# Splitting 28 weight slabs early and pairing two heads in a fused two-block kernel

## The chip, the cores and the metric

The kernel runs on one core of one Trainium2 chip. The metric is the device time of one execution in microseconds. Three executions of the kernel before took 2578.41, 2578.83 and 2579.85 us; their median, 2578.83 us, is the time to compare with.

## The reference

One launch computes two blocks, one after the other, on a sequence of 512 tokens of width 1024, in float32. Cut to what matters here:

```python
for layer in range(2):                                   # block 1
    p = rms_norm(x, norm_g[layer]) @ w_in[layer]
    c_q, c_kv, k_r, gate_a, dil_qkv, gate_b = split(p)
    a = mla_attention(...) * silu(gate_a)
    b = dilated_attention(dil_qkv, cos, sin) * silu(gate_b)
    x = x + concatenate([a, b]) @ w_out[layer]           # output projection
x = rms_norm(x, final_g)
for l in range(2):                                       # block 2
    h = rmsnorm(x) * (1 + scale) + shift
    if l == 0:                                           # recurrent mixers
        p = h @ ab_w_in                                  # 2560 + 1920 columns
        mix = concatenate([hgrn2(p...), rwkv7(p...)]) @ ab_w_out
    else:
        mix = concatenate([fourier(h...), conformer(h...)]) @ cd_w_out
    x = x + gate * mix
    x = x + gate * conv_ffn(rmsnorm(x) * (1 + scale) + shift)
```

The dilated attention has 8 heads of width 64. Each head attends in three groups (dilations 1, 4 and 16), each with its own softmax, and the three results are weighted by a softmax over their log sums.

## The kernel before

Activations lie transposed: features on the 128 partitions, the 512 tokens along the free dimension. A product with a weight matrix goes slab by slab: a slab is 1024 x 128 weights, 512 KB, held as a 128 x 8 x 128 tile. To keep float32 accuracy each operand is split into two parts of the type fp32r (high and low), and three products are summed (`mm3`, L130 to L132). So a slab costs one DMA into `wraw` on SP's queue (L67), a copy on ACT that makes `whi` (L75), a subtraction on DVE that makes `wlo` (L76), and 24 matmuls of 128x512 (`gemm`). `wraw`, `whi` and `wlo` have three buffers each.

Block 1 runs two layers. In each, `block1_mixers` computes the latent attention, then the dilated one. For each pair of dilated heads `operands(p)` makes queries and keys with six gemms, with a rotation of which one multiplication lies on GpSimd (POOL, L591). `attention(p)` then treats the two heads one after the other: for four query tiles, score matmuls into `sc` (L620 to L623), a masked maximum on DVE, an exponential on ACT; then a small exchange of maxima and sums (`ot`, `fa`); then the probabilities are scaled by the factor `fa` on DVE (L663), transposed on TensorE against the identity (`tp`, L669, L671), copied by ACT into `pt` (L674 to L678) and multiplied with the values into `po` (L683, L688).

Each layer ends in `out_proj`: eight gemms with `w_out`, each added to `xT`. In layer 0 each new tile of `xT` is scaled and split into `hh` and `hl` for the next layer's gemms (`Scaled.tile`). In layer 1 the last two gemms go in halves into `pl`, and the norm for block 2 follows (`Norm`).

In block 2 the function `m2` holds the recurrent mixers. Of their slabs, 12 of `w_rw` (the r, k and v of four head pairs) and 16 of `w_hg` go through `gemm` like any other, in between the small matmuls of the recurrences.

A scheduler of the framework puts each engine's instructions in an order while the program is built, by priority and by its own idea of durations; the tile pools add the waits for buffers. On the chip each engine keeps to that order, and so does SP's queue of DMA issues: an instruction that waits holds up all that stands behind it on its engine.

Of the kernel before, what the change touches and what calls it, by code (L numbers as in the profile page):

```python
# [12 lines left out]
ALU = mybir.AluOpType  # L13
# [11 lines left out]
class Ctx:  # L25
# [161 lines left out]
    def out_proj(self, pool, W, k0, mix, xcol, gate=None, norm=None, parts=None):  # L187
        for _ in self.out_proj_steps(pool, W, k0, mix, xcol, gate, norm=norm, parts=parts):
            pass
# [44 lines left out]
def at(x, k):  # L234

    return x[k] if isinstance(x, list) else x[:, k, :]

# [178 lines left out]
def block1_mixers(c, l, nm, mixf, side, w0, fill):  # L416
# [4 lines left out]
    if True:  # L421
# [114 lines left out]
        with ExitStack() as e2:  # L536
# [42 lines left out]
            def operands(p):  # L579

                q0, k0 = (dp.tile([128, 2, S], F32R, name=n, tag=n, bufs=2) for n in ("q0", "k0"))
                k0l = dp.tile([128, S], F32R, name="k0l", tag="k0l", bufs=2)
                qk12 = dp.tile([128, 2, 2, S], F32, name="qk12", tag="qk12", bufs=2)
                qk[p] = q0, k0, k0l, qk12
                for gi in range(3):
                    for j in range(2):
                        ps = c.gemm(I["w_dqk"][l][:, 6 * p + 2 * gi + j], hh, hl)
                        sh = c.t2("shf")
                        xr = c.t2("xr")
                        nc.vector.stream_shuffle(sh, ps, SHUF)  # L590
# [14 lines left out]
                        yield  # L605

            def attention(p):
                q0, k0, k0l, qk12 = qk.pop(p)
                po = c.pz.tile([128, S], F32, name="po", tag="pz")
                for e in range(2):  # L610
                    eb = slice(64 * e, 64 * e + 64)
                    hcol = slice(128 * p + 64 * e, 128 * p + 64 * e + 64)
                    st = dp.tile([128, 2, 2, 4], F32, name="st", tag="st", bufs=2)
                    nm = dp.tile([128, 2, 4], F32, name="nm", tag="nm", bufs=2)
                    pp = dp.tile([128, 4, S], F32, name="pp", tag="pp", bufs=2)
                    for i in range(4):
                        w0 = (0, 64, 192, 256)[i]
                        sc = c.px.tile([128, S], F32, name="sc", tag="px")
                        tq = slice(128 * i, 128 * i + 128)
                        nc.tensor.matmul(sc[:, 0:256], lhsT=q0[:, e, tq], rhs=k0[:, e, w0:w0 + 256], start=True, stop=False)  # L620
                        nc.tensor.matmul(sc[:, 0:256], lhsT=q0[eb, e, tq], rhs=k0l[eb, w0:w0 + 256], start=False, stop=True)
                        for gi in range(2):
                            nc.tensor.matmul(sc[:, 256 + 128 * gi:384 + 128 * gi], lhsT=qk12[eb, 0, gi, tq],  # L623
                                             rhs=qk12[eb, 1, gi, tq], start=True, stop=True)
                        for z in range(2):
                            w = slice(256 * z, 256 * z + 256)
                            nc.vector.tensor_tensor_reduce(pp[:, i, w], in0=sc[:, w], in1=dmask[:, 4 * z or i, :], scale=1.0, scalar=3 * NEG,
                                                           op0=ALU.add, op1=ALU.max, accum_out=st[:, 0, z, i:i + 1])
                        nc.vector.tensor_scalar(nm[:, :, i], st[:, 0, :, i], -0.125, None, op0=ALU.mult)  # L629
                        for z in range(2):  # L630
                            pz = pp[:, i, 256 * z:256 * z + 256]
                            nc.scalar.activation(pz, pz, AF.Exp, bias=nm[:, z, i:i + 1], scale=0.125,  # L632
                                                 accum_out=st[:, 1, z, i:i + 1])

                    ex = dp.tile([128, 2, 2, 128], F32, name="ex", tag="ex", bufs=2)
                    bc = lambda t: t.rearrange("p (z o n) -> p z o n", z=1, o=1).to_broadcast([128, 2, 4, 32])
                    nc.vector.tensor_tensor(ex[:, 0].rearrange("p z (i n) -> p z i n", i=4),
                                            st[:, :, 0, :].rearrange("p z (i o) -> p z i o", o=1).to_broadcast([128, 2, 4, 32]),
                                            bc(sel[:, 0:32]), op=ALU.mult)
                    nc.vector.tensor_tensor(ex[:, 1].rearrange("p z (n r) -> p z r n", r=4),  # L640
                                            st[:, :, 1, :].rearrange("p z (i o) -> p z i o", o=1).to_broadcast([128, 2, 4, 32]),
# [7 lines left out]
                    nc.vector.tensor_tensor(M, st[:, 0], ot[:, 0], op=ALU.max)  # L649
                    nc.vector.tensor_tensor(e1, st[:, 0], M, op=ALU.subtract)  # L650
                    nc.vector.tensor_tensor(e2_, ot[:, 0], M, op=ALU.subtract)
                    nc.scalar.activation(fa[:, 1:3], fa[:, 1:3], AF.Exp, scale=0.125)
                    nc.vector.tensor_tensor(f, e1, st[:, 1], op=ALU.mult)
# [3 lines left out]
                    nc.vector.tensor_tensor(f, f, e1, op=ALU.mult)  # L657

                    pts = []
                    for i in range(4):  # L660
                        for z in range(2):
                            pz = pp[:, i, 256 * z:256 * z + 256]
                            nc.vector.tensor_scalar(pz, pz, f[:, z, i:i + 1], None, op0=ALU.mult)  # L663

                        blocks = (((0, 0, 64, 0), (64, 0, 128, 1)), ((0, 0, 128, 1), (128, 0, 128, 2)),
                                  ((0, 0, 128, 2), (128, 0, 128, 3)), ((192, 64, 64, 0), (64, 0, 128, 3)))[i]
                        tp = c.py.tile([128, 4, 128], F32, name="tp", tag="py")
                        for j, (o, r0, n, vt) in enumerate(blocks):
                            nc.tensor.transpose(tp[0:n, j, :], pp[:, i, o:o + n], c.ident)  # L669
                        for j in range(2):  # L670
                            nc.tensor.transpose(tp[:, 2 + j, :], pp[:, i, 256 + 128 * j:384 + 128 * j], c.ident)  # L671
                        pt = dp.tile([128, 4, 128], F32, name="pt", tag="pt", bufs=4)
                        if i in (1, 2):
                            nc.scalar.activation(pt, tp, AF.Copy)  # L674
                        else:
                            r0 = blocks[0][1]
                            nc.scalar.activation(pt[r0:r0 + 64, 0, :], tp[0:64, 0, :], AF.Copy)
                            nc.scalar.activation(pt[:, 1:4, :], tp[:, 1:4, :], AF.Copy)  # L678
                        pts.append((pt, blocks))
                    for i in range(4):  # L680
                        pt, blocks = pts[i]
                        for j, (o, r0, n, vt) in enumerate(blocks):
                            nc.tensor.matmul(po[eb, 128 * i:128 * i + 128], lhsT=v0[r0:r0 + n, vt, hcol],  # L683
                                             rhs=pt[r0:r0 + n, j, :], start=i == 0 and j == 0, stop=False)
                    for i in range(4):
                        pt, _ = pts[i]
                        for j in range(2):
                            nc.tensor.matmul(po[eb, i::4], lhsT=v12[:, j, i, hcol], rhs=pt[:, 2 + j, :],  # L688
# [123 lines left out]
def rwkv_lora(c, rp, pp, R, hh, hl):  # L812
    nc, W = c.nc, c.ins["w_rw"]
    for ct, n in enumerate(("th", "ad", "gd")):
        ps = c.gemm(W[:, ct], hh, hl)
# [11 lines left out]
def rwkv_g(c, rp, pp, R, P, hh, hl):  # L827

    out = []
    for j, n in enumerate("rkv"):  # L830
        ct = 3 + 3 * P + j
        ps = c.gemm(c.ins["w_rw"][:, ct], hh, hl)
# [396 lines left out]
def hgrn_fill(c, hh, hl, spill):  # L1229

    nc = c.nc
    for h in range(4):
# [13 lines left out]
        for z in (1, 2, 0, 3):  # L1246
            ps = c.gemm(c.ins["w_hg"][:, 4 * h + z], hh, hl)
# [340 lines left out]
def build(tc, I, out):  # L1588
    nc = tc.nc
    with ExitStack() as es:  # L1590
# [60 lines left out]


        for l in range(2):
            ex.close()
            prev = nm
            with ExitStack() as em:
# [15 lines left out]
                c.out_proj(mp, I["w_out"][l], 0, [mixf[:, k] for k in range(KD)], x, norm=nm)  # L1672
            xd = to_dram(xT)
        ea.close()

# [366 lines left out]
```

## Time and profile before

| | |
|---|---|
| median of three executions | 2578.83 us |
| the profiled execution's own time | 2578.49 us |
| its span | 2576.7 us |
| TensorE (PE) busy | 2488.2 us, 97% |
| VectorE (DVE) busy | 1643.1 us, 64% |
| ScalarE (ACT) busy | 1074.9 us, 42% |
| GpSimd (POOL) busy | 220.6 us, 9% |
| HBM read, written | 246.06 MB, 16.52 MB |

The span runs from the first instruction to the last; 1.8 us of the execution lie outside it. PE is the engine that is nearly always busy. The kernel's stages, in us from the span's start: layer 0 from 0 to about 545 (dilated attention 268 to 494, output projection 494 to 545), layer 1 to about 1070 (dilated attention 793 to 1018), the recurrent mixers to about 1600, then the first feed-forward part, the Fourier and convolution mixers and the second feed-forward part. All DMAs of the program are issued on SP's queue.

### The profile page before, as it was taken

Reading aid. Unit: us, or ns where it says so; the run is one execution under the profiler, and the core shown is the slowest. Engines: PE = TensorE matmul, PEld = TensorE weight load, DVE = VectorE, ACT = ScalarE, POOL = GpSimd, SP = SyncE. Lnnn points to the kernel's source line nnn. Section 1 sums busy time; section 2 is a strip of 40 time slices with the busy share of each in tenths; the row PEclk is TensorE's granted clock in tenths of the full one; section 3 lists DMA queues with packets and bytes.
Section 4 is the critical chain, followed back from the end, with each engine's and each line's share of the span. In section 5 each row is a group of like instructions: output and inputs, shape, how many; then the busy total and the mean of one; then the engine's idle time right before and its main releaser. Section 6 shows DMA issues by size and latency. Waiting matters only on the chain. (4 is left out here: it accounts for less than half of the span.)

```text
span 2576.7 us, 38952 instructions
## 1 busy us (share of the span) xinstructions
PE 2488.2 (97%) x15261; PEld 1999.1 (78%) x15261; DVE 1643.1 (64%) x3261; ACT 1074.9 (42%) x1947; POOL 220.6 (9%) x303
## 2 busy tenths in 40 slices
PE   8999999999999999999999888999999989999998
PEld 6769777787697777877677777878888767888887
DVE  5767666647677666576576575786444797543544
ACT  5653333526534335555434652532333424432331
POOL 0000111000001110211000130200000210100000
PEclk9999999999999999999999978999999989999999
DMA  4137121331271213321211422586333403233322
GB/s 150 45 127 241 54 58 56 109 111 40 93 278 58 58 58 95 105 74 51 88 48 55 143 81 82 190 269 209 101 88 122 149 1 97 80 88 103 96 83 81
DMA packets 92023, 265.09 MB, mean 103 GB/s; under 512 B 14528, under 2 KB 27072, under 8 KB 90944
## 3 DMA queue, kind: packets, MB, share of 16 engines
q1 hardware_dynamic: 91840, 262.61, 32.5%
q8 instruction: 120, 1.97, 0.3%
q14 instruction: 63, 0.52, 0.1%
HBM read 246.06 MB, written 16.52 MB: 102 GB/s over the span
## 5 line engine op out<-in xcount | busy, mean ns | idle before, releaser
L75 ACT ACTIVATE whi<-wraw 128x1024 fp32r<-128x1024 f32 (+3 forms) x370 | 348.5, 943 | 774.6 <-PE pg L131 563.7
L130 PE MATMUL pg<-hh,whi 128*128 128x512 f32 x1560 | 629.3, 403 | 7.9 <-ACT whi L124 6.6
L131 PE MATMUL pg<-hl,whi 128*128 128x512 f32 x1560 | 630.9, 404 | 0.0
L132 PE MATMUL pg<-hh,wlo 128*128 128x512 f32 x1560 | 628.0, 403 | 0.0
L76 DVE TENSOR_TENSOR wlo<-wraw,whi 128x1024 fp32r<-128x1024 f32 (+4 forms) x366 | 422.6, 1156 | 284.8 <-ACT whi L75 281.2
L130 PEld LDWEIGHTS pg<-hh,whi 128*128 128x128 f32 x1560 | 295.8, 190 | 88.0 <-ACT whi L124 6.6
L131 PEld LDWEIGHTS pg<-hl,whi 128*128 128x128 f32 x1560 | 295.8, 190 | 76.7 <-issue 8.1
L132 PEld LDWEIGHTS pg<-hh,wlo 128*128 128x128 f32 x1560 | 296.2, 190 | 71.6 <-issue 2.5
L132 PE MATMUL pg<-hidh,wlo 128*128 128x512 f32 (+1 forms) x396 | 145.5, 367 | 0.3 <-DVE wlo L76 0.3
L131 PE MATMUL pg<-hidl,whi 128*128 128x512 f32 (+1 forms) x396 | 145.6, 368 | 0.0
L130 PE MATMUL pg<-hidh,whi 128*128 128x512 f32 (+1 forms) x396 | 145.1, 366 | 0.0
L719 DVE CUSTOM_DVE_ANT_0 adaw<-adaw,sc 128x1024 f32<-128x1024 f32 x96 | 116.3, 1225 | 41.0 <-DMA adaw<-in_ada_w_dram 33.4
L591 POOL TENSOR_TENSOR shf<-shf,roped 128x512 f32<-128x512 f32 x48 | 62.0, 1292 | 532.7 <-ACT whi L75 249.2
L130 PE MATMUL pgv<-whi,hh 128*128 128x512 f32 (+1 forms) x240 | 89.7, 374 | 0.0
L132 PE MATMUL pgv<-whi,hl 128*128 128x512 f32 (+1 forms) x240 | 88.4, 368 | 0.0
L131 PE MATMUL pgv<-wlo,hh 128*128 128x512 f32 (+1 forms) x240 | 88.3, 368 | 0.0
L632 ACT ACTIVATE pp<-pp,nm 128x256 f32<-128x256 f32 x128 | 63.6, 497 | 54.9 <-DVE nm L629 54.8
L130 PEld LDWEIGHTS pg<-hidh,whi 128*128 128x128 f32 x396 | 74.3, 188 | 13.6 <-issue 0.4
L132 PEld LDWEIGHTS pg<-hidh,wlo 128*128 128x128 f32 x396 | 74.4, 188 | 13.1 <-DVE wlo L76 1.0
L131 PEld LDWEIGHTS pg<-hidl,whi 128*128 128x128 f32 x396 | 74.4, 188 | 12.7
L1529 ACT ACTIVATE fu<-fu 128x512 f32<-128x512 f32 x44 | 27.8, 631 | 112.2 <-DVE fu L745 112.2
L231 DVE SCALAR_TENSOR_TENSOR xT<-pg,mod,xT 128x512 f32<-128x512 f32 (+1 forms) x54 | 38.2, 710 | 48.5 <-PE pg L132 48.4
(512 smaller groups left out, 4486.2 us busy)
## 6 DMA issues: line engine op xcount, KB each, us to landing
adaw<-in_ada_w_dram SPq DMA_DIRECT2D x96, 512.0 KB, 4.6
wraw<-in_ffn_up_dram SPq DMA_DIRECT2D x88, 512.0 KB, 3.6
wraw<-in_w_dqk_dram SPq DMA_DIRECT2D x48, 512.0 KB, 3.6
wraw<-in_ffn_down_dram SPq DMA_DIRECT2D x32, 512.0 KB, 3.6
wraw<-in_w_dv_dram SPq DMA_DIRECT2D x24, 512.0 KB, 3.7
wraw<-in_w_gate_dram SPq DMA_DIRECT2D x16, 512.0 KB, 3.7
wraw<-in_w_out_dram SPq DMA_DIRECT2D x16, 512.0 KB, 3.7
wraw<-in_w_hg_dram SPq DMA_DIRECT2D x16, 512.0 KB, 3.7
```

The lines of the kernel that those rows point to most:

```text
L75: nc.scalar.activation(hi, raw, AF.Copy)
L76: (eng or nc.vector).tensor_tensor(lo, raw, hi.bitcast(F32), op=ALU.subtract)
L130: mm(out, lhsT=ah, rhs=bh, start=first, stop=False)
L131: mm(out, lhsT=ah, rhs=bl, start=False, stop=False)
L132: mm(out, lhsT=al, rhs=bh, start=False, stop=last)
L231: self.nc.vector.scalar_tensor_tensor(x, in0=ps, scalar=gate[:, o:o + 1], in1=x, op0=ALU.mult, op1=ALU.add)
L591: nc.gpsimd.tensor_tensor(sh, sh, roped[:, 1, :], op=ALU.mult)
L632: nc.scalar.activation(pz, pz, AF.Exp, bias=nm[:, z, i:i + 1], scale=0.125, accum_out=st[:, 1, z, i:i + 1])
L719: nc.vector.tensor_tensor_reduce(w, in0=w, in1=sc, scale=1.0, scalar=0.0, op0=ALU.mult, op1=ALU.add, accum_out=mod[:, j:j + 1])
L1529: nc.scalar.activation(u, u, AF.Silu)
```

## The change

Two things change together.

**Slabs split ahead.** A new class `Parts` stands for a slab that is split ahead of its use. `make` loads the raw slab into a tile `praw`, splits it into `phi` (ACT) and `plo` (DVE), and stores both to DRAM with two DMAs of 512 KB from GpSimd's queue. The three tiles have two buffers each, in a pool `pre` of their own. `out_proj` in block 1 calls `ahead` after each of its steps, which makes two slabs: 18 of the 28 in layer 0, 10 in layer 1. In `m2` the gemms that use these slabs load `whi` and `wlo` with two DMAs on SP's queue, and ACT and DVE have no part in it.

**Dilated heads.** `attention` treats the two heads of a pair together: their score matmuls, and later their value matmuls, alternate. The factor is no longer multiplied into the probabilities by DVE: ACT makes a diagonal matrix `dg` of it (two per query tile and head), and a matmul with `dg` as moving operand takes the place of the transpose. `pt` now lies in the memory of the probabilities, unused rows are set to zero by GpSimd (L717), and the value matmuls always use all 128 rows. The rotation's multiplication moves from GpSimd to DVE.

```diff
     def wslab(self, src, shape, raw=None, eng=None, out=None):
+        if isinstance(src, Parts):
+            hl = out or [self.w.tile(shape, F32R, name=t, tag=t) for t in ("whi", "wlo")]
+            for t, z in zip(hl, src.parts):
+                nc.sync.dma_start(t.bitcast(F32), z)
+            return hl
...
         for _ in self.out_proj_steps(pool, W, k0, mix, xcol, gate, norm=norm, parts=parts):
-            pass
+            if ahead is not None:
+                ahead()
...
+class Parts:
+    def __init__(self, c, src, name):
+        self.src = src.rearrange("p k n -> p (k n)")
+        self.parts = [c.dram.tile([128, 1024], F32, name=f"{name}{z}") for z in "hl"]
+
+    def make(self, c, pool):
+        raw = pool.tile([128, 1024], F32, name="praw", tag="praw", bufs=2)
+        c.nc.sync.dma_start(raw, self.src)
+        hl = [pool.tile([128, 1024], F32R, name=t, tag=t, bufs=2) for t in ("phi", "plo")]
+        c.split(*hl, raw)
+        for z, t in zip(self.parts, hl):
+            c.nc.gpsimd.dma_start(z, t.bitcast(F32))
...
-                        nc.gpsimd.tensor_tensor(sh, sh, roped[:, 1, :], op=ALU.mult)
+                        nc.vector.tensor_tensor(sh, sh, roped[:, 1, :], op=ALU.mult)
...
+                    sc = [c.px.tile([128, S], F32, name="sc", tag="px") for _ in es]
...
+                    for e, eb, _ in es:
+                        nc.tensor.matmul(sc[e][:, 0:256], lhsT=q0[eb, e, tq], rhs=k0l[eb, w0:w0 + 256], start=False, stop=True)
+                    for gi in range(2):
+                        for e, eb, _ in es:
+                            nc.tensor.matmul(sc[e][:, 256 + 128 * gi:384 + 128 * gi], lhsT=qk12[eb, 0, gi, tq],
                                              rhs=qk12[eb, 1, gi, tq], start=True, stop=True)
...
-                            pz = pp[:, i, 256 * z:256 * z + 256]
-                            nc.vector.tensor_scalar(pz, pz, f[:, z, i:i + 1], None, op0=ALU.mult)
+                            nc.scalar.activation(dg[:, z], c.ident, AF.Copy, scale=fs[e][:, z, i:i + 1])
...
-                            nc.tensor.transpose(tp[:, 2 + j, :], pp[:, i, 256 + 128 * j:384 + 128 * j], c.ident)
+                            mm(tp[:, 2 + j, :], lhsT=pp[e, i][:, 256 + 128 * j:384 + 128 * j], rhs=dg[:, 1], start=True, stop=True)
...
+                for i in range(4):
+                    for j in range(2):
+                        for e, eb, hcol in es:
+                            nc.tensor.matmul(po[eb, i::4], lhsT=v12[:, j, i, hcol], rhs=pts[e, i][0][:, 2 + j, :],
                                              start=False, stop=i == 3 and j == 1)
...
-            ps = c.gemm(c.ins["w_hg"][:, 4 * h + z], hh, hl)
+            ps = c.gemm(c.rparts[15 + 4 * h + z].cut(128), hh, hl)
...
+                pre = c.pool(em, "pre", B)
+                def ahead():
+                    for _ in range(2):
+                        if rtodo:
+                            rtodo.pop(0).make(c, pre)
-                c.out_proj(mp, I["w_out"][l], 0, [mixf[:, k] for k in range(KD)], x, norm=nm)
+                c.out_proj(mp, I["w_out"][l], 0, [mixf[:, k] for k in range(KD)], x, norm=nm, ahead=ahead)
```

What this does to the order of the instructions is seen at three places. First, ACT in the output projection of layer 0, before:

```order
L75 ACTIVATE whi<-wraw 128x1024
L361 ACTIVATE hh<-xT,gv 128x512
L370 ACTIVATE sqa<-xT 128x512
L75 ACTIVATE whi<-wraw 128x1024
L361 ACTIVATE hh<-xT,gv 128x512
L370 ACTIVATE sq<-xT 128x512
L75 ACTIVATE whi<-wraw 128x1024
```

And now (L75 has become L80, L361 L389, L370 L398; L129 is the copy in `split`):

```order
L129 ACTIVATE phi<-praw 128x1024 x2
L80 ACTIVATE whi<-wraw 128x1024
L389 ACTIVATE hh<-xT,gv 128x512
L398 ACTIVATE sqa<-xT 128x512
L129 ACTIVATE phi<-praw 128x1024
L80 ACTIVATE whi<-wraw 128x1024
L129 ACTIVATE phi<-praw 128x1024
L389 ACTIVATE hh<-xT,gv 128x512
L398 ACTIVATE sq<-xT 128x512
L80 ACTIVATE whi<-wraw 128x1024
```

The 18 copies of layer 0 stand between the copies that make `whi` for the projection's gemms and for the first three or four gemms of layer 1. The subtractions on DVE stand likewise.

Second, SP's queue at the same place, before:

```order
L67 DMA wraw<-in_w_out_dram 128x1024 x4
L1620 DMA xT<-in_x_dram 128x4096
L67 DMA wraw<-in_w_out_dram 128x1024 x2
L1605 DMA xd<-xT 128x512
L67 DMA wraw<-in_w_out_dram 128x1024
L1605 DMA xd<-xT 128x512
```

And now (`praw` is the raw slab, loaded in L254):

```order
L67 DMA wraw<-in_w_out_dram 128x1024 x4
L1662 DMA xT<-in_x_dram 128x4096
L254 DMA praw<-in_w_rw_dram 128x1024 x2
L67 DMA wraw<-in_w_out_dram 128x1024 x2
L254 DMA praw<-in_w_rw_dram 128x1024 x2
L67 DMA wraw<-in_w_out_dram 128x1024
L1647 DMA xd<-xT 128x512 x2
L254 DMA praw<-in_w_rw_dram 128x1024
L67 DMA wraw<-in_w_out_dram 128x1024
```

The loads of weights for the gemms now stand behind loads of `praw`, which wait for the splits of earlier slabs. The 36 stores of layer 0 stand on POOL, with nothing else among them.

Third, PE in the attention of the first pair of heads, before:

```order
L669 MATMUL tp<-c_ident,pp 128x128 x2
L671 MATMUL tp<-c_ident,pp 128x128 x2
L669 MATMUL tp<-c_ident,pp 64x128
L669 MATMUL tp<-c_ident,pp 128x128
L671 MATMUL tp<-c_ident,pp 128x128 x2
L683 MATMUL po<-pt,v_1512 64x128 x7
L688 MATMUL po<-pt,v_1513 64x128 x8
```

And now, where the value matmuls of the two heads alternate (L725, L730):

```order
L709 MATMUL tp<-dg,pp 128x128 x2
L711 MATMUL tp<-dg,pp 128x128 x2
L725 MATMUL po<-pp,v_1568 64x128 x2
L709 MATMUL tp<-dg,pp 64x128
L709 MATMUL tp<-dg,pp 128x128
L711 MATMUL tp<-dg,pp 128x128 x2
L725 MATMUL po<-pp,v_1568 64x128 x6
L135 MATMUL pg<-hh,whi 128x512
L725 MATMUL po<-pp,v_1568 64x128
L730 MATMUL po<-pp,v_1569 64x128 x16
```

The numbers of matmuls are the same for a pair of heads (32 `tp`, 32 `po`). Of the `po`, the 16 of L730 stand in one run, and those of L725 stand in pairs between groups of `tp`. The score matmuls of the two heads stand in pairs for the first query tile alone; for the other three the order puts a gemm's matmul between the heads.

## Rows read from the trace of the kernel before

**Rows 1.** The page's span and its line for PE.

```profile
span 2576.7 us, 38952 instructions
...
PE 2488.2 (97%) x15261; PEld 1999.1 (78%) x15261; DVE 1643.1 (64%) x3261; ACT 1074.9 (42%) x1947; POOL 220.6 (9%) x303
```

**Rows 2.** Windows of four stages: busy us (instructions) by engine, PEclk, DMA share, GB/s.

```profile
268.00:494.00 226.00, 223.87 (x1168) 173.04 (x1169) 150.63 (x425) 99.60 (x242) 24.53 (x19) 0.98 0.20 60
486.00:559.00 73.00, 73.00 (x334) 60.36 (x333) 40.37 (x59) 28.27 (x40) 0.00 (x0) 0.98 0.46 149
1011.00:1052.00 41.00, 41.00 (x188) 33.71 (x187) 24.93 (x38) 19.26 (x29) 0.00 (x0) 1.00 0.57 181
1088.00:1480.00 392.00, 371.95 (x4921) 290.02 (x4920) 261.10 (x581) 197.17 (x357) 45.23 (x82) 0.99 0.24 76
```

**Rows 3.** Windows of a stage with many DMAs, and of its fullest five us.

```profile
176.00:260.00 84.00, 84.00 (x360) 76.44 (x359) 60.93 (x87) 28.60 (x34) 5.19 (x4) 1.00 0.68 232
215.00:220.00 5.00, 5.00 (x23) 5.00 (x23) 4.65 (x7) 0.97 (x2) 0.00 (x0) 1.00 1.02 391
```

**Rows 4.** PE's timeline, dilated attention of layer 0: start, us, line, operands, count.

```profile
277.97 0.38 PE L621 MATMUL sc<-k0l,q 64*128 64x256 f32 x1
278.19 0.60 PE L623 MATMUL sc<-qk 64*128 64x128 f32 x4
289.49 0.38 PE L669 MATMUL tp<-c_ident,pp 128*64 128x128 f32 x2
289.70 0.38 PE L671 MATMUL tp<-c_ident,pp 128*128 128x128 f32 x2
292.11 2.03 PE L683 MATMUL po<-pt,v 128*64 128x128 f32 x14
293.98 1.91 PE L688 MATMUL po<-pt,v 128*64 128x128 f32 x16
```

**Rows 5.** PE's timeline, latent attention (L532) and recurrent mixers.

```profile
108.11 3.65 PE L532 MATMUL po<-ptm,vm 128*64 128x512 f32 x14
1424.99 2.01 PE L1103 MATMUL psg<-U,T 128*128 128x128 f32 x16
1428.54 0.67 PE L1128 MATMUL psz<-U,G 64*64 64x128 f32 x16
```

**Rows 6.** ACT's lines in 268 to 494 us: count, busy us, mean ns, idle before.

```profile
L674 ACT ACTIVATE pt<-tp 128x512 f32<-128x512 f32 x16 | 9.5, 593 | 5.6 <-PE tp L671 5.6
L677 ACT ACTIVATE pt<-tp 64x128 f32<-64x128 f32 x16 | 4.3, 266 | 9.9 <-PE tp L671 9.7
```

**Rows 7.** SP's queue: the two loads of xT ahead of the projections.

```profile
486.22 0.33 SPq L1620 DMA_DIRECT2D xT<-in_x_dram  x1
1010.94 0.33 SPq L1620 DMA_DIRECT2D xT<-xd  x1
```

**Rows 8.** Timeline of ACT, then DVE, in the projections of both layers.

```profile
521.49 1.06 ACT L75 ACTIVATE whi<-wraw 128x1024 fp32r<-128x1024 f32 x1 [3.30 <-issue]
526.99 1.06 ACT L75 ACTIVATE whi<-wraw 128x1024 fp32r<-128x1024 f32 x1 [3.30 <-issue]
561.08 0.69 DVE L460 TENSOR_TENSOR cf<-pg,rbx 128x512 f32<-128x512 f32 x1 [3.47 <-PE pg L132]
1051.71 1.06 ACT L75 ACTIVATE whi<-wraw 128x1024 fp32r<-128x1024 f32 x1 [3.29 <-issue]
1052.80 1.23 DVE L76 TENSOR_TENSOR wlo<-wraw,whi 128x1024 fp32r<-128x1024 f32 x1 [0.23 <-ACT whi L75]
```

**Rows 9.** DMA issues: operation, count, KB each, median us to landing.

```profile
adaw<-in_ada_w_dram SPq DMA_DIRECT2D x96, 512.0 KB, 4.6
```

**Rows 10.** PE's waits in 268 to 494 us: total, times, longest.

```profile
PE tp L669 <- DVE pp L663: 1.8, 3, 0.6
```

**Rows 11.** A window with PE waiting; a gemm's matmul at a low clock.

```profile
1575.00:1600.00 25.00, 18.15 (x80) 13.89 (x79) 11.68 (x26) 6.27 (x11) 0.00 (x0) 0.73 0.11 26
...
284.06 0.63 PE L132 MATMUL pg<-hh,wlo 128*128 128x512 f32 x1
```

More of the change, by code (lines that the diff above doesn't have):

```diff
@@ L184, in rms_bcast, with out_proj @@
         return rb
[L187 removed]
+    def out_proj(self, pool, W, k0, mix, xcol, gate=None, norm=None, parts=None, ahead=None):
         for _ in self.out_proj_steps(pool, W, k0, mix, xcol, gate, norm=norm, parts=parts):
[L189 removed]
+            if ahead is not None:
+                ahead()
     def out_proj_steps(self, pool, W, k0, mix, xcol, gate=None, done=None, norm=None, parts=None):
@@ L236, in at, with cut @@
     return x[k] if isinstance(x, list) else x[:, k, :]
+class Parts:
[9 more added lines that the diff above has]
+            c.nc.gpsimd.dma_start(z, t.bitcast(F32))
+    def cut(self, n, k0=0, k1=None):
+        v = Parts.__new__(Parts)
+        v.parts = [z.rearrange("p (k n) -> p k n", n=n)[:, k0:k1] for z in self.parts]
+        return v
 class Norm:
@@ L609, in attention @@
                 po = c.pz.tile([128, S], F32, name="po", tag="pz")
[L610 to L623, printed above, removed]
+                es = [(e, slice(64 * e, 64 * e + 64), slice(128 * p + 64 * e, 128 * p + 64 * e + 64)) for e in range(2)]
@@ new lines, in attention @@
+                st = [dp.tile([128, 2, 2, 4], F32, name="st", tag="st", bufs=2) for _ in es]
+                nm = [dp.tile([128, 2, 4], F32, name="nm", tag="nm", bufs=2) for _ in es]
+                pp = {}
+                for i in range(4):
+                    w0 = (0, 64, 192, 256)[i]
+                    sc = [c.px.tile([128, S], F32, name="sc", tag="px") for _ in es]
+                    tq = slice(128 * i, 128 * i + 128)
+                    if i % 2 == 0:
+                        for e, _, _ in es:
+                            t = dp.tile([128, 2, S], F32, name="pp", tag="pp", bufs=6)
+                            pp[e, i], pp[e, i + 1] = t[:, 0], t[:, 1]
+                    for e, eb, _ in es:
+                        nc.tensor.matmul(sc[e][:, 0:256], lhsT=q0[:, e, tq], rhs=k0[:, e, w0:w0 + 256], start=True, stop=False)
+                    for e, eb, _ in es:
+                        nc.tensor.matmul(sc[e][:, 0:256], lhsT=q0[eb, e, tq], rhs=k0l[eb, w0:w0 + 256], start=False, stop=True)
+                    for gi in range(2):
+                        for e, eb, _ in es:
+                            nc.tensor.matmul(sc[e][:, 256 + 128 * gi:384 + 128 * gi], lhsT=qk12[eb, 0, gi, tq],
@@ L635, in attention @@
-                    ex = dp.tile([128, 2, 2, 128], F32, name="ex", tag="ex", bufs=2)
+                            pz = pp[e, i][:, 256 * z:256 * z + 256]
+                            nc.scalar.activation(pz, pz, AF.Exp, bias=nm[e][:, z, i:i + 1], scale=0.125,
+                                                 accum_out=st[e][:, 1, z, i:i + 1])
+                fs = []
+                for e, _, _ in es:
+                    ex = c.t2("ex").rearrange("p (o z n) -> p o z n", o=2, z=2)
                     bc = lambda t: t.rearrange("p (z o n) -> p z o n", z=1, o=1).to_broadcast([128, 2, 4, 32])
@@ L676, in attention @@
                             r0 = blocks[0][1]
+                            nc.gpsimd.memset(pt[64 - r0:128 - r0, 0, :], 0.0)
                             nc.scalar.activation(pt[r0:r0 + 64, 0, :], tp[0:64, 0, :], AF.Copy)
                             nc.scalar.activation(pt[:, 1:4, :], tp[:, 1:4, :], AF.Copy)
[L679 to L688, printed above, removed]
+                        pts[e, i] = pt, blocks
+                for i in range(4):
+                    for j in range(2):
+                        for e, eb, hcol in es:
+                            pt, blocks = pts[e, i]
+                            nc.tensor.matmul(po[eb, 128 * i:128 * i + 128], lhsT=v0[:, blocks[j][3], hcol], rhs=pt[:, j, :],
+                                             start=i == 0 and j == 0, stop=False)
+                for i in range(4):
+                    for j in range(2):
+                        for e, eb, hcol in es:
+                            nc.tensor.matmul(po[eb, i::4], lhsT=v12[:, j, i, hcol], rhs=pts[e, i][0][:, 2 + j, :],
                                              start=False, stop=i == 3 and j == 1)
@@ L812, in rwkv_lora @@
 def rwkv_lora(c, rp, pp, R, hh, hl):
-    nc, W = c.nc, c.ins["w_rw"]
+    nc = c.nc
     for ct, n in enumerate(("th", "ad", "gd")):
-        ps = c.gemm(W[:, ct], hh, hl)
+        ps = c.gemm(None, hh, hl)
         o = c.t2("rlo") if n == "th" else R["gd"] if n == "gd" else rp.tile([128, S], F32, name=n)
@@ L831, in rwkv_g @@
         ct = 3 + 3 * P + j
-        ps = c.gemm(c.ins["w_rw"][:, ct], hh, hl)
+        ps = c.gemm(c.rparts[ct].cut(128), hh, hl)
         o = rp.tile([128, S], F32, name=n, tag=n, bufs=2)
@@ L1650, in build @@
         ap = c.pool(ea, "ada", B)
+        c.rparts = {k: Parts(c, I["w_rw"][:, k], f"rw{k}") for k in range(3, 15)} | {15 + k: Parts(c, I["w_hg"][:, k], f"hg{k}") for k in range(16)}
+        rtodo = list(c.rparts.values())
         for l in range(2):
```

37 lines of the change are left out of this document (20 added, 17 removed).

## The prediction

> **What bounds the kernel now.** I read the page's busy lines first. TensorE (PE) works for 2488.2 of a span of 2576.7 us, 97% [rows 1], so only two things can move the time by much: work taken from PE or given to it, and new waits that make it idle. Then I read windows by stage [rows 2]. In the dilated attention of layer 0 (226 us) PE is busy for 223.9, and a window over layer 1's reads the same. In the output projections it is busy for all of 73 and 41 us. Only the recurrent mixers leave room: 371.95 of 392 us, 20 idle. Last I read the DMA share, since the change sends 28 slabs to DRAM and back. In the projections it is 0.46 and 0.57 already, at 149 and 181 GB/s [rows 2].
>
> **The output projections: new traffic ahead of the gemms' weights.** In layer 0 ACT makes 18 `phi`, and `phi` has two buffers, so the copy for slab 17 can't start until slab 15's store has landed. ACT runs in order, and behind that copy stands the one that makes `whi` for the fourth gemm of layer 1; DVE's `wlo` stands likewise, and SP's weight loads stand behind those of `praw`. So the stores decide when PE gets its weights.
>
> By when must slab 17 be ready? That gemm starts at 561.1, when DVE evicts the third [rows 8]. Its `whi` and `wlo` take 1.06 and 1.23 us, and the copy ahead of them another 1.06 [rows 8]; so the copy must start at 557.7. Traffic starts with the load of `xT` at 486.2 [rows 7]. That leaves 71.5 us. In it the old traffic moves 149 GB/s x 71.5 = 10.7 MB. New are 17 raw loads of 0.524 MB (8.9 MB) and the two stores of 15 slabs, 1.05 MB each (15.7 MB): 35.3 MB in all, or 494 GB/s. The fullest 5 us of the run moved 391 GB/s, at a share of 1.02; a longer stretch moved 232 at 0.68, so 341 if full [rows 3]. At 391 the 35.3 MB take 90.3 us, 19 too many; at 341 they take 103.5, 32 too many. PE has nothing else to do there, since all its operands come through `whi`. I take the middle, 25.
>
> Layer 1 has 10 slabs ahead of the projection's last `whi` at 1051.7 [rows 8], so the copy of slab 10 must start at 1050.6. From 1010.9 [rows 7] that is 39.7 us. Old traffic 181 x 39.7 = 7.2 MB, ten raw loads 5.2, stores of eight slabs 8.4: 20.8 MB. At 391 GB/s 53.2 us, 13 late; at 341 61.0, 21 late. I take 17. Together **+42**, with ends at 32 and 53. Beyond them: at the rates of these very windows, full (149/0.46 = 324, 181/0.57 = 318), it would be +63, and +0 if the trace's fullest 5 us are no limit.
>
> No trace here shows a store from GpSimd's queue, and if such stores had bandwidth of their own, layer 0 would need only 19.6 MB in 71.5 us and no stall would come. The Trainium skill speaks against that (DMA: Bandwidth & Descriptors, section Issuing engines are not separate DMA queues): transfers issued by different engines end up on the same 16 DMA engines and interleave. By this rule the +42 stands; without it this term is 0, the first rival below. No run here shows it.
>
> The split instructions themselves (28 x 1.06 us on ACT, 28 x 1.23 on DVE) are hidden: in the first window ACT works 28.3 of 73 us and DVE 40.4 [rows 2].
>
> **The dilated attention.** Per layer and pair of heads (eight in all) PE's work changes in three places. A row of the timeline lasts about 0.17 us beyond its last matmul's slot: L669 lasts 0.38 and the next row starts after 0.21 [rows 4]. I take that off.
>
> - Transposes. A pass of 128 columns took 0.105 us and one pass makes a transpose [rows 4]. A plain float32 matmul is two records: L688 shows 16 for the 8 matmuls of one head. With 128 weight columns a record takes (2.01 - 0.17) / 16 = 0.115 [rows 5]. 256 transposes, 26.9 us, become 512 records, 58.9: **+32**.
> - Values. L683 took 0.133 a record and L688 0.109 [rows 4], for 256 records each 62.0 us. L532 already alternates heads: 14 records of 512 columns at 0.249 [rows 5], where four times L688's 0.109 would be 0.436. So a pair takes 0.57 of it, 0.062 a record. I give L730 (one run of 16 matmuls) that, and L725, in pairs between `tp` groups, half the gain, 0.09: 38.9 us, **-23**.
> - Scores. Only the first of four query tiles has the heads side by side. Per pair of heads that is two L621 of 0.22 and eight records of L623 at 0.107 [rows 4]; with 43% off, 0.55 us: **-4**.
>
> Sum +5. Ends: +32 if pairs gain nothing, and -18 if each value record takes the 0.031 of L1128, where four quadrants of the array alternate [rows 5].
>
> The Trainium skill names a price against this change (TensorE: Matmul & The Clock Gate, section Terms): transpose mode is four times faster for float32 than a matmul. The rows say 0.105 against two records of 0.115, a factor of 2.2. By the page the term would be 3 x 26.9 = +81 and the time 49 us longer than forecast; the measurement decides, and it gets the small chance below.
>
> Waits. PE waited 1.8 us in all for L663's scaling in layer 0 [rows 10]; with layer 1, -3.6. In its place comes a chain: per query tile and head ACT makes two `dg` (0.27 each, from the 128-column L677) and a copy of 0.59 [rows 6], 1.1 us, beside PE's four `tp` and two `po` of 1.2, with two buffers each. Late next is ACT: I take 0.5 us per pair of heads, +4 (0 to 13). DVE loses L663 and gains the rotation's multiplication; at 150.6 of 226 us busy [rows 2] it hides either. GpSimd's zeroing comes off the path. So the stage costs **+5** in all.
>
> **The recurrent mixers.** ACT loses 28 x 1.06 = 30 of its 197 us and DVE 28 x 1.23 = 34 of its 261 [rows 2]. Some of PE's 20 idle us go with it: a third, **-7**. Ends: all 20, or +8 if loads that now write `whi` and `wlo` directly, three deep where raw and split slabs together were six, come late behind a store of `spill` on SP's queue. The 14.7 MB more in 392 us are 37 GB/s on top of 76: hidden.
>
> **Sum.** 2576.7 + 42 + 5 - 7 = 2616.7 us of span. The profiled execution took 2578.49, 1.8 more than its span, and the median is 0.3 above that: **2618.8**, rounded to 2618.
>
> **Rivals.**
>
> *The stores hide* (16%). A pair of slabs needs two copies, a subtraction and a landing: 2 x 1.06 + 1.23 + 4.6 us (a 512 KB load among many in flight [rows 9]) = 8.0; the pace allowed is 71.5 us less about 11 for the first load, over 8 pairs, 7.6. So on latency alone it nearly fits, and if the engines move more than 391 GB/s the projections lose nothing. The limit is a loop of 7.6 us. Quick loads also give the mixers more, -12: 2576.7 + 0 + 5 - 12 + 2.1 = 2572, faster than before. Against it: the share of 1.02 at 391 GB/s.
>
> *The clock falls in the gaps* (12%). Where PE was busy for 18.15 of 25 us the granted clock was 0.73, and a gemm's matmul at the low level lasts 0.63 [rows 11]. At 1.2 instead of 2.4 GHz a gemm takes about 5 us more than its 5.5 [rows 8]. Of some 18 gemms in the two stretches half might run so; less the 2.3 us each waits anyway, 9 x 2.7 = +24: 2643. For it: stalls come at every gemm. Against: each is short.
>
> *Pairs gain nothing* (11%): the dilated term is 27 worse, 2645. For it: the two passes of each matmul stand together, so heads alternate only every second record. Against: L532 stands the same way.
>
> *Transposes four times cheaper than matmuls* (2%): 2667.
>
> **Range and chances.** The forecast has 56%, with its own range from 2603 (projections +28) to 2640 (projections +63). 3% is left for small sums of low ends. I call 0.2%, 5 us, what this kernel's measurement can tell from no change. Faster than 2573.7: most of the first rival and the 3%, 0.14. Within: the rest of the first rival and the forecast's low tail, 0.08. Slower: 0.78. The range for 8 in 10 goes from 2573 to 2652.
>
> **What would show it.** In the changed profile the windows of both projections have a DMA share near 1 and PE idle, with `whi` waiting behind `phi`, and `phi` for a DMA. L709 and L711 have twice the records of L669 and L671; L730's records stand at about 0.06 us. PE's idle time in the mixers falls below 20 us. I am wrong if PE stays busy through the projections, or if the DMA engines move well over 400 GB/s.

## The result and the profile after

The changed kernel took **2602.28 us** in the median (2598.16 to 2616.68, four runs), beside 2578.62 for the kernel before: a ratio of 1.0102, 95% interval 1.0079 to 1.0125. The forecast was 2618, slower. The profiled execution took 2600.94 us.

The page answers to [rows 1]: on balance PE is 1.5 us busier and the span 22.5 longer, so the time went into waiting. (Less work in one stage and slower work in another nearly cancel in the 1.5, as the stages show.)

```profile
span 2599.2 us, 39767 instructions
...
PE 2489.7 (96%) x15517; PEld 2004.0 (77%) x15517; DVE 1608.3 (62%) x3181; ACT 1115.5 (43%) x2075; POOL 193.5 (7%) x343
```

To see where, I cut both spans at the same events: the first eviction into `xT` of layer 0's projection; the last `cf` of layer 1 (it follows the last gemm that layer 0's slabs can delay); the load of `xT` from `xd`; the first `u` of block 2's norm; the load of `xT` from `xn` behind the mixers. In us:

| stage | before | after | difference | forecast |
|---|---|---|---|---|
| to the end of layer 0's dilated attention | 499.7 | 495.6 | -4.1 | with layer 1: +5 |
| layer 0's projection to the last `cf` | 72.6 | 94.8 | +22.2 | +25 |
| layer 1's attentions | 438.6 | 433.7 | -4.9 | |
| layer 1's projection | 57.5 | 73.1 | +15.6 | +17 |
| recurrent mixers | 495.5 | 490.0 | -5.5 | -7 |
| the rest | 1012.8 | 1012.0 | -0.8 | 0 |

Windows of the changed kernel: layer 0's dilated attention, both projections, the mixers (columns as in [rows 2], to which they answer).

```profile
264.00:489.90 225.90, 225.37 (x1321) 175.91 (x1320) 138.30 (x386) 120.12 (x307) 3.18 (x16) 1.00 0.21 64
...
495.60:590.40 94.80, 79.77 (x323) 64.16 (x322) 53.42 (x66) 38.63 (x46) 18.60 (x35) 0.89 0.98 385
1024.10:1097.20 73.10, 64.32 (x331) 55.04 (x328) 43.66 (x69) 35.14 (x49) 10.76 (x21) 0.88 0.89 333
...
1097.20:1587.20 490.00, 459.03 (x5499) 365.22 (x5499) 300.28 (x694) 226.48 (x440) 86.69 (x128) 0.97 0.31 107
```

The same three stages (projections, mixers) of the kernel before:

```profile
499.70:572.30 72.60, 72.60 (x323) 59.73 (x322) 34.55 (x50) 22.46 (x30) 0.00 (x0) 0.98 0.42 134
1010.90:1068.40 57.50, 57.50 (x316) 50.13 (x315) 32.48 (x59) 25.07 (x39) 0.00 (x0) 0.97 0.47 149
...
1068.40:1563.90 495.50, 464.26 (x5499) 367.71 (x5499) 332.70 (x722) 253.00 (x468) 88.18 (x128) 0.95 0.24 76
```

In layer 0's projection PE is idle for 94.80 - 79.77 = 15.0 us, and its work takes 79.77 instead of 72.60, 7.2 more, at a mean clock of 0.89 instead of 0.98. In layer 1 it is 8.8 idle and 6.8 more at 0.88. So of 37.8 us 23.8 are waiting and 14.0 a lower clock. Ten-us windows show both beside full DMA engines (share 1.02 or 1.03), and one window over the whole stretch shows the rate that lasted, 400 GB/s:

```profile
540.00:550.00 10.00, 5.29 (x18) 3.91 (x17) 5.94 (x7) 4.19 (x5) 2.13 (x4) 0.85 1.03 415
550.00:560.00 10.00, 4.19 (x19) 3.43 (x17) 6.09 (x9) 4.30 (x5) 1.59 (x3) 0.84 1.02 405
560.00:570.00 10.00, 10.00 (x39) 8.62 (x39) 5.61 (x13) 3.17 (x3) 2.66 (x5) 0.62 1.02 404
...
500.00:585.00 85.00, 69.97 (x281) 56.19 (x280) 47.51 (x60) 35.82 (x42) 17.00 (x32) 0.88 1.01 400
```

PE's timeline at one of the waits: after 4.71 us without work the matmuls of the next gemm start 0.43 us apart and last 0.63, as at the low clock of [rows 11], for some 3 us; then they last 0.40 again. So a wait costs something again after it has ended.

```profile
541.32 0.40 PE L137 MATMUL pg<-mh,wlo 128*128 128x512 f32 x1
546.43 0.47 PE L135 MATMUL pg<-hh,whi 128*128 128x512 f32 x1 [4.71 <-DVE xT L235]
...
547.34 0.63 PE L135 MATMUL pg<-hh,whi 128*128 128x512 f32 x1
547.77 0.63 PE L136 MATMUL pg<-hl,whi 128*128 128x512 f32 x1
...
550.62 0.40 PE L137 MATMUL pg<-hh,wlo 128*128 128x512 f32 x1
```

The releaser named there, an eviction into `xT`, did come late. `pg` has two buffers, so this gemm, the first of layer 1, needs the buffer of the last gemm but one, which ended at 536.0. That buffer's eviction ran at 545.61. In DVE's order it stands behind two `plo`, and both waited for the store of an earlier `plo`. PE started 0.14 us after the eviction had ended. The gemm's own weights had long been there: loads land after at most 9.6 us, this one was issued at 512.80, and its `wlo` is the row at 541.01.

```profile
541.01 1.22 DVE L81 TENSOR_TENSOR wlo<-wraw,whi 128x1024 fp32r<-128x1024 f32 x1
544.47 1.22 DVE L130 TENSOR_TENSOR plo<-praw,phi 128x1024 fp32r<-128x1024 f32 x1 [2.23 <-DMA rw11l<-plo]
545.61 0.68 DVE L235 TENSOR_TENSOR xT<-xT,pg 128x512 f32<-128x512 f32 x1
```

Nearly all of PE's idle time in the two projections is of this kind. In layer 0 its waits are for evictions, and for `sqa`, which follows the last of them on DVE; in layer 1 evictions give 8.6 of 8.8 us. PE's waits in 480 to 620 us:

```profile
PE pg L135 <- DVE xT L235: 9.2, 3, 4.7
PE pst L406 <- DVE sqa L400: 5.8, 1, 5.8
```

What holds `plo` up are `phi` (17.0 us of DVE's waits in 490 to 600 us) and the stores of `plo` (five waits, 11.0 us). What holds `phi` up are the raw loads, which land after 7.4 us in the median, where a slab of `w_out` took 3.7 before. ACT's waits in 480 to 620 us name these loads, and no load of weights for the gemms:

```profile
ACT phi L129 <- DMA praw<-in_w_rw_dram: 25.0, 9, 5.1
...
ACT phi L129 <- DMA praw<-in_w_hg_dram: 10.6, 4, 3.9
```

In the dilated attention PE is as busy as before. Its groups by form over both layers, columns: count, busy us, mean ns, idle before:

```profile
L711 PE MATMUL tp<-dg,pp 128*128 128x128 f32 x256 | 39.1, 275 | 0.0
L709 PE MATMUL tp<-dg,pp 128*128 128x128 f32 x192 | 36.8, 301 | 0.0
L657 PE MATMUL sc<-qk 64*128 64x128 f32 x256 | 36.0, 277 | 1.1
L725 PE MATMUL po<-pp,v 128*64 128x128 f32 x256 | 30.3, 294 | 0.0
...
L730 PE MATMUL po<-pp,v 128*64 128x128 f32 x256 | 17.4, 274 | 0.0
L709 PE MATMUL tp<-dg,pp 128*64 128x128 f32 x64 | 13.0, 285 | 0.0
```

and of the kernel before:

```profile
L623 PE MATMUL sc<-qk 64*128 64x128 f32 x256 | 43.2, 279 | 0.6
L688 PE MATMUL po<-pt,v 128*64 128x128 f32 x256 | 30.6, 272 | 0.0
L683 PE MATMUL po<-pt,v 128*64 128x128 f32 x192 | 29.5, 283 | 0.0
...
L671 PE MATMUL tp<-c_ident,pp 128*128 128x128 f32 x128 | 24.5, 273 | 0.0
...
L669 PE MATMUL tp<-c_ident,pp 128*128 128x128 f32 x96 | 21.1, 274 | 0.0
...
L683 PE MATMUL po<-pt,v 64*64 64x128 f32 x64 | 13.7, 295 | 0.0
L669 PE MATMUL tp<-c_ident,pp 128*64 128x128 f32 x32 | 8.7, 272 | 3.7 <-DVE pp L663 3.7
```

The transposes (`tp`) went from 54.3 to 88.9, the values (`po`) from 73.8 to 47.7; every score group got shorter too, L623 (now L657) by 7.2. The 3.7 us of waiting for L663 are gone, and no wait for `dg` has come.

### The profile page after: what moved, and what is told of

Its sections match the earlier page's. It is cut to its first block, busy times and chain, and to the rows that moved or that the text cites. A ratio compares the mean times of both kernels' runs of the same rounds, so it can differ in the third digit from the quotient of the medians.

```text
span 2599.2 us, 39767 instructions
## 1 busy us (share of the span) xinstructions
PE 2489.7 (96%) x15517; PEld 2004.0 (77%) x15517; DVE 1608.3 (62%) x3181; ACT 1115.5 (43%) x2075; POOL 193.5 (7%) x343
## 5 line engine op out<-in xcount | busy, mean ns | idle before, releaser
L80 ACT ACTIVATE whi<-wraw 128x1024 fp32r<-128x1024 f32 (+3 forms) x342 | 318.5, 932 | 674.8 <-PE pg L136 544.6
L81 DVE TENSOR_TENSOR wlo<-wraw,whi 128x1024 fp32r<-128x1024 f32 (+3 forms) x338 | 360.8, 1069 | 261.7 <-ACT whi L80 258.5
L135 PE MATMUL pg<-mh,whi 128*128 128x512 f32 x164 | 66.8, 408 | 9.8 <-DVE xT L235 8.0
```

Source lines behind the costliest of these rows:

```text
L135: mm(out, lhsT=ah, rhs=bh, start=first, stop=False)
```

## The experiments

The theory, from the trace: the 16 DMA engines are full in the projections, so slabs come late (**volume**). The rival: `phi` and `plo` stand ahead of `whi` and `wlo` in ACT's and DVE's order, in a loop of two buffers (**order**). Each kernel was timed against the kernel before on its own chip; ratios with 95% intervals:

| kernel | median, us | ratio to before |
|---|---|---|
| heads_only | 2571.74 | 0.9981 (0.9970 to 0.9992) |
| slabs_only | 2619.30 | 1.0163 (1.0149 to 1.0177) |
| traffic | 2610.74 | 1.0134 (1.0120 to 1.0148) |
| pre4 | 2617.52 | 1.0151 (1.0137 to 1.0165) |
| half | 2580.52 | 1.0025 (1.0015 to 1.0036) |
| stores_sp | 2638.80 | 1.0249 (1.0223 to 1.0274) |
| quiet_w | 2628.58 | 1.0219 (1.0201 to 1.0237) |
| pairs_ident | 2559.65 | 0.9945 (0.9932 to 0.9957) |
| ident_k64 | 2533.85 | 0.9827 (0.9807 to 0.9847) |
| one_slab | 2567.46 | 0.9960 (0.9945 to 0.9975) |
| after_again | 2608.20 | 1.0118 (1.0101 to 1.0134) |

**heads_only.**

```diff
-                c.out_proj(mp, ..., x, norm=nm, ahead=ahead)
+                c.out_proj(mp, ..., x, norm=nm)
-            ps = c.gemm(c.rparts[15 + 4 * h + z].cut(128), hh, hl)
+            ps = c.gemm(c.ins["w_hg"][:, 4 * h + z], hh, hl)
```

> The paired dilated heads alone; the slabs are split live in the mixers as before. By the milestones of the changed profile the two dilated stages gave 4.1 and 4.5 us, so 2578.6 - 8.6 = 2570 us, and both projections and the mixers should take what they took before. By the sum of the prediction (+5) it would be 2584.

The pairs alone gain a little: the two attentions took 4.5 and 4.9 us less than before, the projections 72.7 and 56.0. The forecast's +5 for this part had the wrong sign.

**slabs_only.** The changed kernel with the attention (and the rotation on GpSimd) of the kernel before.

> The early slabs alone, with the dilated heads one after the other as before. If the two parts add up: projections +22.2 and +15.4, mixers -5.5, so 2578.6 + 32 = 2611 us. If the pairs and the slabs disturb each other (both use ACT, DVE and GpSimd), it differs from the changed kernel less the gain of the pairs by over 5 us.

The projections took 95.4 and 73.7 us, as in the changed kernel, and the profiled span was 2616.0. With heads_only's (2567.0) the halves add up to 2616.0 + 2567.0 - 2576.7 = 2606, between the 2599.2 and 2609.0 of the two profiled executions of the changed kernel.

**traffic.**

```diff
-        raw = pool.tile(..., tag="praw", bufs=2)
+        raw = pool.tile(..., tag="praw", bufs=6)
-        c.split(*hl, raw)
-        for z, t in zip(self.parts, hl):
-            c.nc.gpsimd.dma_start(z, t.bitcast(F32))
+        for z in self.parts:
+            c.nc.gpsimd.dma_start(z, raw)
```

> Paired heads; during the projections the same 28 slabs are loaded and twice stored by the same queues, from six raw buffers, but nothing is split: no phi and no plo stand in ACT's and DVE's order, and the mixers split their slabs live. Theory volume (the 16 DMA engines are full): the same bytes delay the same weights, projections about +37, so 2570 + 37 = 2607 us. Theory order (whi and wlo stand behind phi and plo, a loop of two buffers): no such loop, so 2570 to 2575 us.

Volume holds: 39 us above heads_only without a single `phi`. In this kernel's projection PE has nothing to do for a whole window while the engines stay full, then runs at 0.65 and 0.52:

```profile
540.00:550.00 10.00, 0.00 (x0) 0.00 (x0) 1.08 (x1) 1.06 (x1) 1.69 (x4) 0.50 1.03 419
550.00:560.00 10.00, 6.05 (x15) 4.30 (x15) 5.27 (x8) 3.54 (x5) 2.11 (x4) 0.65 1.03 419
560.00:570.00 10.00, 10.00 (x39) 8.81 (x40) 2.59 (x10) 1.06 (x1) 2.10 (x4) 0.52 1.03 416
```

The path to PE is another one than in the changed kernel, though. Here the weights themselves come late, and DVE's evictions stand behind the `wlo` made of them. ACT's wait for them in 490 to 600 us:

```profile
ACT whi L80 <- DMA wraw<-in_w_in_dram: 30.1, 4, 17.1
```

So the bytes are enough to cost this much without the splits. Not taken apart are the bytes and the order of SP's queue: the loads of weights stand behind those of `praw` here too, the first of `w_in` was issued at 531.21 instead of 512.80, and no run put them ahead.

**pre4.** `bufs=4` instead of 2 for `praw`, `phi` and `plo`.

> The changed kernel with four buffers each for the raw, high and low slabs instead of two. Theory volume: at the last gemms two slabs more may still wait for their stores, 2.1 MB or 5 us at 410 GB/s per layer, so 2602 - 10 = 2592 us, with the DMA share still near 1. Theory order: the loop is twice as loose and nearly all of the 37 us go, 2565 to 2575 us.

Both missed: it isn't faster than the changed kernel (ratio 1.0151, beside 1.0102 and 1.0118 of that kernel's two timings), and layer 0's projection took 101.5 us instead of 94.8. A looser loop puts more slabs on the full engines sooner: SP's order now has six loads of `praw` before the fifth slab of `w_out` instead of two, and layer 1's last weight loads, issued behind its own slabs, took 14.5 us to land (8.5 in the changed kernel). PE's longest waits in layer 0's projection are now for weights and no longer for evictions:

```profile
PE pg L135 <- ACT whi L80: 21.2, 2, 16.7
```

So the small buffers held the damage down: with a looser loop the full engines reach PE by another path. The order theory alone, without full engines, doesn't explain this.

**half.** One slab per step, and only those with odd numbers.

> Paired heads; only 14 of the 28 slabs (every second one) are split early, one per step of the projections, nine in layer 0 and five in layer 1; the other 14 are split live in the mixers. Theory volume has a threshold: by the sum of the prediction layer 0 needs 10.7 + 9 x 0.524 + 7 x 1.05 = 22.8 MB in 71.5 us, 319 GB/s, layer 1 7.2 + 2.6 + 3.2 = 13.0 MB in 39.7 us, 327 GB/s; both fit under 410, so no stall: 2568 to 2573 us. If every early slab costs its share of the 39 us: 2571.7 + 20 - 3 = 2589 us.

Between the two: by the ratios about 11 us over heads_only. Layer 1's projection lost 1.5 us, layer 0's 8.3, though its bytes fit on the average. They come bunched:

```profile
500.00:540.00 40.00, 35.80 (x144) 28.47 (x143) 26.23 (x31) 20.35 (x25) 7.44 (x14) 0.91 1.03 413
540.00:580.00 40.00, 40.00 (x176) 33.07 (x175) 15.42 (x25) 8.09 (x9) 0.00 (x0) 0.91 0.39 126
```

Read so, the threshold is there, but it has to be asked of each stretch, not of the whole stage.

**stores_sp.** `c.nc.sync.dma_start` for the stores instead of `c.nc.gpsimd.dma_start`.

> The changed kernel with the stores issued on SP's queue instead of GpSimd's. Theory volume: the bytes are the same, so at best the same 2602 us; and SP's queue runs in order, so weight loads stand behind stores that wait for a split, which makes it slower: 2602 to 2640 us. If it is GpSimd's queue that holds the slabs up, it becomes faster: under 2590 us.

Slower, as volume with SP's order has it. SP's stores wait for the split, the weight loads behind them wait too, and PE waits once for 37.4 us:

```profile
PE pg L135 <- ACT whi L80: 40.4, 2, 37.4
```

GpSimd's queue did not hold the slabs up; it kept the waiting stores off SP's queue. That transfers from both queues share the same engines, as the Trainium skill says (DMA: Bandwidth & Descriptors, section Issuing engines are not separate DMA queues), agrees with the trace of traffic: the engines were at a share of 1.03 with loads from SP and stores from GpSimd together.

**quiet_w.**

```diff
                 for _ in range(6 + QL if p == 0 else 6):
                     next(steps, None)
+                    nst += 1
+                    if nst * 7 // 12 > (nst - 1) * 7 // 12 and c.rtodo:
+                        c.rtodo.pop(0).make(c, None)
```

`make` here uses `wslab`'s own tiles, and out_proj gets no `ahead`.

> Paired heads; all 28 slabs are split early, but in the dilated attentions (14 in each layer, after 14 of the 24 gemms there), through the buffers of the gemms (wraw, whi, wlo), stored by GpSimd's queue. Theory volume: there the DMA engines are idle for 80%, 22 MB in 200 us are 110 GB/s more, hidden; the projections take what they took before and the mixers keep their gain of 5: 2566 us. If the split, the store or the later double loads cost something by themselves wherever they stand: 2575 to 2610 us.

A miss. The projections are back at 72.6 and 56.0, as volume has it, but the attentions took 27.6 and 22.6 us longer than in heads_only. Here it is the order, as far as the rows show it: ACT's `whi` waits until the store has read the shared buffer, and the exponentials of the scores stand behind it (the first row below is 26.2 us in heads_only). ACT's waits in 260 to 520 us:

```profile
ACT pp L664 <- DVE nm L661: 37.5, 18, 7.1
...
ACT whi L80 <- DMA rw5h<-whi: 6.5, 1, 6.5
```

PE was idle for 11.5 us of the 262.8 from 260 to the end of layer 0's attention. Its work in that stage took 251.3 us at a mean clock of 0.93, in heads_only 234.7 at 1.00, so here too slower work came with the waits. Whether buffers of their own for these slabs would help wasn't tried.

**pairs_ident.** heads_only with the scaling and the transposes of before:

```diff
-                            nc.scalar.activation(dg[:, z], c.ident, AF.Copy, scale=fs[e][:, z, i:i + 1])
+                            nc.vector.tensor_scalar(pz, pz, fs[e][:, z, i:i + 1], None, op0=ALU.mult)
-                            mm(tp[0:n, j, :], lhsT=pp[e, i][:, o:o + n], rhs=dg[:, 0], start=True, stop=True)
+                            nc.tensor.transpose(tp[0:n, j, :], pp[e, i][:, o:o + n], c.ident)
```

> Paired heads without early slabs, but the probabilities are scaled on DVE and transposed against the identity as before, instead of by matmuls with a scaled identity (dg). If the transposes are the 34.6 us that the changed profile shows for L709 and L711 over L669 and L671: 2571.7 - 34.6 = 2537 us, and up to 2545 with waits for DVE's scaling coming back (3.6 us before) . If the transposes cost nothing because something else bounds the dilated stage: 2572 us.

About 9 us by the ratios, instead of 35; in the profiles the two attentions took 13.9 us less than in heads_only. The waits of PE show what ate the rest: 18.4 us for GpSimd's zeroing (`pp` L717), eight times. The timeline at the first of them, DVE, then GpSimd, then PE:

```profile
291.07 3.50 DVE L705 TENSOR_SCALAR pp<-pp,fa 128x256 f32<-128x256 f32 x13
...
291.70 3.00 POOL L717 MEMSET pp<- 64x128 f32 x1 [137.23 <-DVE pp L705]
...
294.76 0.69 PE L725 MATMUL po<-pp,v 128*64 128x128 f32 x2 [2.58 <-POOL pp L717]
```

**ident_k64.** The same without the zeroing.

```diff
-                            nc.gpsimd.memset(pt[64 - r0:128 - r0, 0, :], 0.0)
-                            nc.tensor.matmul(po[eb, ...], lhsT=v0[:, blocks[j][3], hcol], rhs=pt[:, j, :],
+                            nc.tensor.matmul(po[eb, ...], lhsT=v0[r0:r0 + n, vt, hcol], rhs=pt[r0:r0 + n, j, :],
```

> Paired heads without early slabs, scaled on DVE and transposed against the identity, and without GpSimd's zeroing: the first value block of query tiles 0 and 3 uses 64 weight rows again instead of 128 with zeros. In the run with the zeroing PE waited 18.4 us for GpSimd's memset, which took up to 3.16 us instead of 0.2. If that wait goes: 2559.7 - 18 = 2542 us. If the 64-row matmuls lose the gain of the pairs, or another wait (DVE's scaling) ends as late: 2550 to 2560 us.

**2533.85 us, faster than both kernels**: 1.7% below before. The two attentions took 38.1 us less than in heads_only. The transposes of this kernel are half as many records, 54.9 us instead of 88.8, which by these groups is 34 of the 38; where the other 4 come from wasn't followed:

```profile
L711 PE MATMUL tp<-c_ident,pp 128*128 128x128 f32 x128 | 24.4, 273 | 0.0
...
L709 PE MATMUL tp<-c_ident,pp 128*128 128x128 f32 x96 | 21.4, 277 | 0.0
...
L709 PE MATMUL tp<-c_ident,pp 128*64 128x128 f32 x32 | 9.1, 284 | 0.0
```

**one_slab.** All gemms of the mixers read the parts of one slab.

> The changed kernel with a single slab split early; all 28 gemms of the mixers load the two parts of this one (27 slabs are left out of the computation). So the projections carry no traffic worth naming and the mixers read as many bytes as in the changed kernel: the mixers' term by itself. If it is the -5.5 us of the changed profile: 2571.7 - 5.5 = 2566 us. If that was only the granted clock of one execution (0.955 against 0.944 over the stage): 2570 to 2573 us. The forecast had -7.

2567.46 us, and PE's idle time in the mixers is 489.20 - 457.89 = 31.3 us:

```profile
1055.60:1544.80 489.20, 457.89 (x5501) 363.94 (x5500) 300.75 (x695) 226.97 (x440) 86.83 (x128) 0.97 0.31 107
```

Its ratio and that of heads_only, timed at different times, have overlapping intervals. The profile decides no better, since heads_only has 33.5 us idle there and a clock that differs; a gain of some us is possible, not shown.

**after_again.**

> The changed kernel unchanged, once more, for how far its executions lie apart: the runs so far went from 2598 to 2617 us. If the two halves of the change add up (slabs alone +42, pairs alone -5), its median lies at 2612 rather than 2602; otherwise at 2602 again.

2608.20 us: between the two. Its stages are those of the first run but for the mixers, 500.5 us instead of 490.0, with PE idle for 30.5 and a mean clock of 0.94 instead of 0.97:

```profile
1095.30:1595.80 500.50, 469.98 (x5499) 371.61 (x5499) 300.65 (x694) 227.30 (x440) 85.84 (x128) 0.94 0.31 104
```

So 10 us between two executions of one kernel are the clock of the mixers alone, where PE waits often.

## Why the prediction was right, point by point

**The projections, +42: measured +37.8, the cause right, its path and make-up wrong.** That bytes fill the DMA engines and PE starves is shown by traffic and heads_only. Two sizes in it were off and offset each other. The rate: +25 and +17 mean 366 GB/s, between 391 and a rate scaled up from a stretch that wasn't full; 400 lasted for 85 us. The 391 was a misreading besides, for it isn't the fullest stretch of the kernel before:

```profile
155.00:160.00 5.00, 5.00 (x28) 3.91 (x25) 3.17 (x10) 2.54 (x6) 0.00 (x0) 1.00 1.02 413
```

With 400, and 403 over layer 1's 1040 to 1086 us, the forecast's own sum gives 35.3 / 0.400 - 71.5 = 16.8 and 20.8 / 0.403 - 39.7 = 11.9; measured are 15.0 and 8.8 of waiting. And the clock, put into a rival of its own as another +24, is no alternative but comes with the waiting: 14.0. Both hold, each smaller than written. That their sum came within 4 us of a term made of waiting alone is luck.

**"The stores decide when PE gets its weights"** names the path, and that was wrong. PE didn't wait for weights in either projection. It waited for evictions, which stand behind `plo` in DVE's order; the forecast has `wlo` there and left the eviction out. The stores have a part in it, 11.0 us of DVE's waits, and the raw loads another, 35.6 us of ACT's. Both are slow on full engines. The two buffers of `phi` were a brake and not the cause, by pre4.

**The dilated attention, +5: measured -9.0.** Transposes +34.6 (forecast +32), values -26 (-23), the wait for L663 -3.7 (-3.6): these stand. L730 is the clearest: 0.06 us a record was forecast, and the first line below has 31 records in 2.01 us, 0.059 by the reading of [rows 4].

```profile
304.76 2.01 PE L730 MATMUL po<-pp,v 128*64 128x128 f32 x31
...
269.55 0.39 PE L654 MATMUL sc<-k0l,q 64*128 64x256 f32 x2
```

Two terms failed. The scores, by the groups of all three lines, lost 11.8 us instead of 4 (and `ot` 1.2). The heads stand side by side in the first query tile alone, as I had counted: the later rows of four L657 last 0.60 us, as L623's in [rows 4]. But there the second head is nearly free, where 43% off the pair was assumed: the two L654 above, one of each head, last 0.39 us together, and one L621 lasted 0.38. How the whole of the 11.8 comes about wasn't followed; rows overlap at their ends, so a sum of busy time by groups isn't all time on the path. And the chain of ACT, +4, never came: among PE's waits no row names `dg` or `tp`.

**The mixers, -7: the step failed, whatever the 5.5 in the profile.** PE was idle for 31.2 us before and 31.0 after over the whole stage, so no third of the idle time went. The shorter stage goes with the clock, 0.97 against 0.95; the second execution had 0.94 and took 5.0 us more than before.

**The rivals.** "The stores hide" fell with the share of 1.01 over 85 us. Its condition, that the engines move more than 391 GB/s, was met, with 416 in the fullest ten us, but that wasn't enough. The forecast's own sign against itself, well over 400 GB/s, came near for the same reason. "Pairs gain nothing" fell with heads_only and L730. The transposes at four times the price fell too: 88.8 us in heads_only against 54.9 in ident_k64 for the same tiles is a factor of 1.6. The rule of the Trainium skill (TensorE: Matmul & The Clock Gate, section Terms) isn't borne out for 128 columns in this kernel, though its direction is: the transposes by matmul cost 34 us, and ident_k64 has them back.

**The sum.** Against the profiled execution the forecast's 40 us more are 22.5: 14 of the 17.5 us between them are the dilated term, whose sign was wrong, and 4 the projections; the mixers and the rest nearly cancel.

## What to carry to other kernels

Before moving transfers into a stage, add its bytes to those already there and compare with the rate that the engines hold when full, for every stretch of some ten us; an average over the stage hides a bunch. Ask of every instruction that waits for such a transfer what stands behind it on its engine: here it was the evictions that free the buffers of the matmuls, not only the weights. Where TensorE waits, add the slower clock behind each wait. A quiet DMA is no room if the copies stand in a chain on ACT. And a change of several parts is worth taking apart: here the pairing of heads was good, and the early slabs and the transposes by matmul hid it.

## What the runs showed of the hardware that was not expected

GpSimd's memset of 64x128 took 0.20 us alone and 3.00 us beside 13 `tensor_scalar` instructions of DVE: it ended when their row ended, 291.70 + 3.00 against 291.07 + 3.50. The Trainium skill has a lock on a port pair that DVE and GpSimd share (SBUF — State Buffer, section Who interferes with whom), held for an instruction at a time; the trace agrees with such a lock, though here it would have been held over instructions that stood back to back. In the changed kernel, where ACT scales, all 32 of these memsets took 0.20 us.

The DMA engines moved 400 GB/s for 85 us at a share of 1.01, and 413 to 420 in windows at 1.03, with loads and stores mixed. The kernel before reached 413 as well, but for 5 us.
